# A gated linear unit on one core: handing out row pairs to partitions in another order

## The chip, the cores and the metric

The kernel runs on one core of one Trainium2 chip. The metric is device time in microseconds (us), the median of several executions; lower is better. Before the change it is 934.0 us, the median of three runs from 933.32 to 934.62 us.

## The reference

```python
def setup_inputs():
    return {
        "x": np.random.randn(8192, 8192).astype(np.float32),
    }

def reference(x: np.ndarray) -> np.ndarray:
    a, b = np.split(x, 2, axis=-1)
    return a * (1 / (1 + np.exp(-b)))
```

A row of x has 8,192 float32 values (32 KiB). Its second half is put through a sigmoid and multiplied into its first half, which gives a row of 4,096 values (16 KiB). Each output row depends on one input row alone, so it doesn't matter which partition of the on-chip memory a row passes through, as long as it is stored to the place that belongs to it. The kernel must read 268.44 MB and write 134.22 MB.

## The kernel before

A tile is 256 rows. Each of the 128 partitions holds two neighbouring rows of it (R = 2), called a row pair below: 64 KiB of input, 32 KiB of output. There are 32 tiles and two slots each for input and output.

```python
    R = 2
    SLOTS = 2
    n_tiles = n_rows // (P * R)
    x_t = x.rearrange("(n p r) m -> n p (r m)", p=P, r=R)
    out_t = out.rearrange("(n p r) m -> n p (r m)", p=P, r=R)

    pool = ctx.enter_context(tc.tile_pool(name="io", bufs=1))
    xs = [pool.tile([P, R * n_cols], fp32, name=f"x_sb{k}") for k in range(SLOTS)]
    os = [pool.tile([P, R * half], fp32, name=f"o_sb{k}") for k in range(SLOTS)]
    # ... cut: helpers for the waits
    for i in range(n_tiles):
        # ... cut: bookkeeping
        rows = xs[i % SLOTS].rearrange("p (r h m) -> p r h m", r=R, h=2)
        packed = os[i % SLOTS].rearrange("p (r m) -> p r m", r=R)

        load = nc.sync.dma_start(out=xs[i % SLOTS], in_=x_t[i])
        # ... cut
        if 0 < i < n_tiles - 1:
            parts = [(slice(0, R), slice(0, half))]
        else:
            w = half // 2
            parts = [
                (slice(r, r + 1), slice(c * w, (c + 1) * w)) for r in range(R) for c in range(2)
            ]
        def store(cols):
            ins = nc.scalar.dma_start(out=out_t[i, :, cols], in_=os[i % SLOTS][:, cols])
            now["stores"].append(ins)

        chunks = []
        for k, (r, c) in enumerate(parts):
            b = rows[:, r, 1, c]
            sig = nc.scalar.activation(out=b, in_=b, func=SIG)
            mul = nc.vector.tensor_mul(out=packed[:, r, c], in0=rows[:, r, 0, c], in1=b)
            # ... cut: which waits are kept
            chunks.append(slice(r.start * half + c.start, r.start * half + c.stop))
            if i == n_tiles - 1 and k > 0:
                store(chunks[k - 1])
        store(chunks[-1] if i == n_tiles - 1 else slice(0, R * half))
```

Loads are issued from SyncE, stores from ScalarE. A load goes into the slot of the tile two before it, so it waits for that tile's multiply. The last tile is stored in four parts of 1 MiB; every other tile is one load of 8 MiB and one store of 4 MiB. What is cut only decides which semaphore waits are written out, moves the first load ahead of the start-up, and shortens the closing sequence; the change touches none of it.

Of the kernel before, what the change touches and what calls it, by code (L numbers as in the profile page):

```python
# [1 line left out]

# [4 lines left out]


def _tiles(ctx, tc, x, out):

    nc = tc.nc
    P = nc.NUM_PARTITIONS  # L20
    DEP = mybir.DependencyInfo(mybir.DependencyClass.Sync, mybir.DependencyReason.DATA)
    fp32 = mybir.dt.float32
    SIG = mybir.ActivationFunctionType.Sigmoid

    n_rows, n_cols = x.shape
    half = n_cols // 2
    R = 2
    SLOTS = 2
    n_tiles = n_rows // (P * R)
    x_t = x.rearrange("(n p r) m -> n p (r m)", p=P, r=R)  # L30
    out_t = out.rearrange("(n p r) m -> n p (r m)", p=P, r=R)

    pool = ctx.enter_context(tc.tile_pool(name="io", bufs=1))
    xs = [pool.tile([P, R * n_cols], fp32, name=f"x_sb{k}") for k in range(SLOTS)]
    os = [pool.tile([P, R * half], fp32, name=f"o_sb{k}") for k in range(SLOTS)]

    def implied(later, *earlier):
        for e in earlier:
            tc.declare_no_dep(later.ins, e.ins, reason="follows from the waits that are kept")

    gone = [{k: [] for k in ("loads", "sigs", "muls", "stores")} for _ in range(SLOTS)]
    last_stores = [[] for _ in range(SLOTS)]
    for i in range(n_tiles):
        old = gone[i % SLOTS]
        freed = last_stores[i % SLOTS]
        now = {k: [] for k in old}
# [4 lines that stand above are left out]
        implied(load, *old["loads"], *old["sigs"])  # L51
        now["loads"].append(load)
# [6 lines that stand above are left out]
                (slice(r, r + 1), slice(c * w, (c + 1) * w)) for r in range(R) for c in range(2)  # L59
            ]  # L60
        def store(cols):
            ins = nc.scalar.dma_start(out=out_t[i, :, cols], in_=os[i % SLOTS][:, cols])  # L62
            now["stores"].append(ins)

        chunks = []
# [4 lines that stand above are left out]
            implied(sig, *old["sigs"], *old["muls"], *old["loads"])  # L70
            implied(mul, *old["muls"], *old["loads"], *now["loads"])
            by_sigmoid = i % 2 == 1 and len(parts) == 1
            implied(mul, *(s for s in old["stores"] if by_sigmoid or s not in freed))
            if by_sigmoid:
                for s in freed:
                    tc.add_manual_dep(sig.ins, s.ins.name, DEP, reason="frees the output slot")
            tc.keep_in_program_order(sig)
            now["sigs"].append(sig)
            now["muls"].append(mul)
# [4 lines that stand above are left out]
        for s in now["stores"]:  # L84
            implied(s, *old["loads"], *old["sigs"], *old["muls"], *now["loads"], *now["sigs"])
        for k in old:
            old[k] += now[k]
        last_stores[i % SLOTS] = now["stores"]


def _launch_early(nc):

    SP = mybir.EngineType.SP
    entry, body = (b.instructions for b in nc.main_func.blocks[:2])
    load = next(i for i in body if i.engine == SP and i.opcode == "DMACopy")
    assert not load.sync_info.on_wait
    body.remove(load)
    where = next(k for k, i in enumerate(entry) if i.engine == SP and i.opcode == "Drain")  # L100
    entry.insert(where, load)


def _close_on_sync(nc):

    SP, POOL = mybir.EngineType.SP, mybir.EngineType.Pool  # L110
    ACT = mybir.EngineType.Activation
    block = nc.main_func.blocks[2].instructions
    waits = block[0]
    assert waits.engine == SP and waits.opcode == "Drain" and len(waits.sync_info.on_wait) > 1
    pool = [i for i in block if i.engine == POOL]
    drain1, gather1, release1, reset, clear, drain2, gather2, release2 = pool
    assert reset.is_reset_sema and clear.opcode == "ISA"
    others = [i for i in block[1:] if i.engine != POOL]
    arrive = [i for i in others[: len(others) // 2] if i.opcode == "Drain"]
    assert len(arrive) == 4  # L120
    body = nc.main_func.blocks[1].instructions
    last = [i for i in body if i.engine == ACT and i.opcode == "DMACopy"][-1].sync_info.on_update[0].id
    final = [w for w in waits.sync_info.on_wait if w.id == last]
    assert len(final) == 1

    def event(engine, wait, update=()):
        return mybir.InstEventSemaphore(
            name=nc.get_next_instruction_name(),
            engine=engine,
            debug=waits.debug,  # L130
            sync_info=mybir.SyncInfo(on_wait=[wait], on_update=list(update)),
        )

    n = len(block)
    for lo, hi in ((reset.reset_range_start, last), (last + 1, reset.reset_range_stop)):
        if lo < hi:
            nc.gpsimd.sem_clear(range(lo, hi))
    clears = block[n:]
    assert clears and all(i.opcode == "ISA" for i in clears)
    back = mybir.SyncUpdate(  # L140
        sync_type="semaphore",
        id=last,
        ant_name=final[0].ant_name,
        update_mode="sem-sub-imm",
        update_value=final[0].wait_value,
        update_reg=None,
    )
    block[:] = [
        *arrive,
        drain1,  # L150
        gather1,
        *(event(POOL, w) for w in waits.sync_info.on_wait if w.id != last),
        reset,
        *clears,
        drain2,
        event(SP, final[0], [back]),
    ]


@with_exitstack  # L160
def kernel(
    ctx: ExitStack,
    tc: tile.TileContext,
    x: bass.AP,
    out: bass.AP,
):
    nc = tc.nc
    with ExitStack() as pools:
        _tiles(pools, tc, x, out)
    tc.close()  # L170
    tc.compile()
    _launch_early(nc)
    _close_on_sync(nc)


# [1 line left out]
_INS = ['x']  # L177
_OUTS = [((8192, 4096), 'float32')]


# [23 lines left out]
```

## Time and profile before

| | before |
|---|---|
| time, median of 3 | 934.0 us |
| span of the profiled execution | 931.7 us |
| sigmoid on ScalarE, full tile of 128 x 8,192 | 7.03 us (30 of them) |
| multiply on VectorE, full tile | 8.69 us (30 of them) |
| load, from issue to landing (median of 32) | 42.2 us |
| store of 4 MiB, from issue to landing (median of 31) | 34.7 us |
| chain that ended last | DMA 73%, DVE 15%, ACT 12% |

In the page of a profile, a busy digit is the busy share of one of 40 equal slices of the span, in tenths. The DMA row is the mean over the core's 16 DMA engines. q1 is the queue of the loads and q10 that of the stores: number of packets, megabytes, and the time that the packets took as a share of 16 engines over the span. The chain is followed back from the last instruction: at each step to what released it. A wait line names who waited for whom, the total in us, how often, and the longest.

### The profile page before, as it was taken

Reading aid. Unit: us, or ns where it says so; the run is one execution under the profiler, and the core shown is the slowest. Engines: PE = TensorE matmul, PEld = TensorE weight load, DVE = VectorE, ACT = ScalarE, POOL = GpSimd, SP = SyncE. Lnnn points to the kernel's source line nnn. Section 1 sums busy time; section 2 is a strip of 40 time slices with the busy share of each in tenths; the row PEclk is TensorE's granted clock in tenths of the full one; section 3 lists DMA queues with packets and bytes.
Section 4 is the critical chain, followed back from the end, with each engine's and each line's share of the span. In section 5 each row is a group of like instructions: output and inputs, shape, how many; then the busy total and the mean of one; then the engine's idle time right before and its main releaser. Section 6 shows DMA issues by size and latency. Waiting matters only on the chain.

```text
span 931.7 us, 247 instructions
## 1 busy us (share of the span) xinstructions
DVE 278.7 (30%) x38; ACT 227.1 (24%) x39; POOL 0.2 (0%) x4
## 2 busy tenths in 40 slices
DVE  0333213333133331233312333123331233312333
ACT  1323330233311333113331133311333113332033
POOL 0000000000000000000000000000000000000000
DMA  9999999999999999999999999999999999999999
GB/s 405 428 450 428 422 456 405 450 428 428 450 418 438 428 436 442 428 428 450 447 408 428 442 459 428 413 460 411 450 428 425 453 408 447 428 428 450 425 430 405
DMA packets 9649, 402.67 MB, mean 432 GB/s; under 512 B 1072, under 2 KB 1072, under 8 KB 1072
## 3 DMA queue, kind: packets, MB, share of 16 engines
q1 hardware_dynamic: 4608, 268.44, 66.6%
q10 hardware_dynamic: 5040, 134.22, 33.4%
q14 instruction: 1, 0.01, 0.0%
HBM read 268.44 MB, written 134.22 MB: 432 GB/s over the span
## 4 chain that ended last, share of the span: by engine, by line
DMA 73%; DVE 15%; ACT 12%; issue 0%; ACTq 0%
DMA x_sb<-in_x_dram 73%; DVE o_sb L69 15%; ACT x_sb L68 12%; ACTq L62 0%; ACTq L68 0%
## 5 line engine op out<-in xcount | busy, mean ns | idle before, releaser
L69 DVE TENSOR_TENSOR o_sb<-x_sb 128x8192 f32<-128x8192 f32 (+1 forms) x38 | 278.7, 7344 | 647.1 <-ACT x_sb L68 647.1
L68 ACT ACTIVATE x_sb<-x_sb 128x8192 f32<-128x8192 f32 (+1 forms) x38 | 225.8, 5952 | 695.6 <-DMA x_sb<-in_x_dram 694.4
L68 ACT ACT_TABLE_LOAD x1 | 1.3, 1283 | 0.8 <-PEq L188 0.8
L188 POOL MEMSET const-bfloat16-1.0<- 128x1 bf16 x1 | 0.1, 102 | 0.0
L188 POOL MEMSET const-uint8-127<- 128x1 uint8 x1 | 0.1, 102 | 0.0
L188 POOL MEMSET const-float32-0.0<- 128x1 f32 x1 | 0.1, 99 | 0.2 <-issue 0.2
L188 POOL MEMSET const-float32-1.0<- 128x1 f32 x1 | 0.1, 99 | 0.0
## 6 DMA issues: line engine op xcount, KB each, us to landing
out_dram<-o_sb ACTq DMA_DIRECT2D x31, 4096.0 KB, 34.7
out_dram<-o_sb ACTq DMA_DIRECT2D x4, 1024.0 KB, 5.6
x_sb<-in_x_dram SPq DMA_DIRECT2D x32, 42.2
```

The costliest lines, as they stand in the source:

```text
L68: sig = nc.scalar.activation(out=b, in_=b, func=SIG)
L69: mul = nc.vector.tensor_mul(out=packed[:, r, c], in0=rows[:, r, 0, c], in1=b)
L188: nc = _bacc.Bacc("TRN2", target_bir_lowering=False, num_devices=1)
```

## The change

Within a tile, partition p takes row pair 16 (p mod 8) + p div 8 where it took row pair p. Loads and stores use the same rule, so every output row comes out where it did. With p = 8 a + b, the partition's row pair is 16 b + a: partitions 0 to 7 hold row pairs 0, 16, 32, ..., 112, partitions 8 to 15 hold 1, 17, ..., 113, and so on.

The aim: the transfers are done by 16 DMA engines. If engine a serves the eight partitions from 8 a on, one after the other, then the sixteen engines read sixteen neighbouring row pairs at a time, one contiguous megabyte of memory, and step on to the next megabyte together[...]. The access pattern of the tensor in memory gets one dimension more for it, 16 x 8 x run where it was 128 x run; that of the on-chip tile stays 128 x run.

```diff
@@ -26,9 +26,10 @@
     half = n_cols // 2
     R = 2
     SLOTS = 2
+    ENGINES = 16
     n_tiles = n_rows // (P * R)
-    x_t = x.rearrange("(n p r) m -> n p (r m)", p=P, r=R)
-    out_t = out.rearrange("(n p r) m -> n p (r m)", p=P, r=R)
+    x_t = x.rearrange("(n b a r) m -> n a b (r m)", a=ENGINES, b=P // ENGINES, r=R)
+    out_t = out.rearrange("(n b a r) m -> n a b (r m)", a=ENGINES, b=P // ENGINES, r=R)
 
@@ -59,7 +60,7 @@
         def store(cols):
-            ins = nc.scalar.dma_start(out=out_t[i, :, cols], in_=os[i % SLOTS][:, cols])
+            ins = nc.scalar.dma_start(out=out_t[i, :, :, cols], in_=os[i % SLOTS][:, cols])
             now["stores"].append(ins)
```

## The prediction

> **What bounds the kernel now.** I read the page first: how busy each engine is, the DMA rows and the queue table.
>
> ```profile
> DVE 278.7 (30%) x38; ACT 227.1 (24%) x39; POOL 0.2 (0%) x4
> ...
> DMA  9999999999999999999999999999999999999999
> ...
> DMA packets 9649, 402.67 MB, mean 432 GB/s; under 512 B 1072, under 2 KB 1072, under 8 KB 1072
> ## 3 DMA queue, kind: packets, MB, share of 16 engines
> q1 hardware_dynamic: 4608, 268.44, 66.6%
> q10 hardware_dynamic: 5040, 134.22, 33.4%
> ```
>
> The compute engines are idle more than two thirds of the time; the 16 DMA engines are never idle. The queue table gives the cost of one packet. The load queue's 4,608 packets are 32 loads x (128 + 16): 4,096 packets of data, 64 KiB each (268.44 MB / 4,096), one to a partition, and 16 tiny ones per load. They take 0.666 x 16 x 931.7 us = 9,929 engine-us, or 2.424 us each. The store queue moves as many row pairs at 32 KiB: 0.334 x 16 x 931.7 / 4,096 = 1.216 us. The trace's packet records are just as flat: the median load packet is 2.418 us and 98% lie between 2.418 and 2.440; every 32 KiB store packet is 1.213 to 1.216. That is 65,536 B / 2.418 us = 27.1 GB/s for each engine, x 16 = 434 GB/s.
>
> Next the busy time by windows two tiles long (columns: window, its length, DVE, ACT, POOL, PEclk, DMA share, GB/s), and the chain that ended last (start, length, what):
>
> ```profile
> 116.00:174.00 58.00, 17.43 (x3) 14.06 (x2) 0.00 (x0) 1.00 1.00 434
> 582.00:640.00 58.00, 17.17 (x3) 14.06 (x2) 0.00 (x0) 1.00 1.00 433
> ```
>
> ```profile
> 102.88 7.04 ACT x_sb L68
> ...
> 109.94 8.70 DVE o_sb L69
> 118.66 42.09 DMA x_sb<-in_x_dram
> ...
> 160.84 7.04 ACT x_sb L68
> ```
>
> Two tiles take 160.84 - 102.88 = 57.96 us, 28.98 each. One tile costs an engine 8 load and 8 store packets, 8 x 2.418 + 8 x 1.213 = 29.05 us. The two agree: a tile lasts as long as an engine's sixteen packets, and the chain's sigmoid and multiply lie beside other transfers. Last the waits:
>
> ```profile
> ACT x_sb L68 <- DMA x_sb<-in_x_dram: 694.4, 32, 22.3
> ...
> SPq L50 <- DVE o_sb L69: 859.9, 30, 31.7
> ```
>
> ScalarE waits some 22 us per tile for a load, so compute has that much slack; and a load is issued only when the multiply two tiles back has freed its slot, which leaves roughly one to two loads in the queue. So the time is (packets per engine) x (time of a packet), and the change can act only through the packet's time or the spread of packets over engines.
>
> [...]
>
> **The change, part by part.** Removed and added: no instruction, byte or packet. A run in DRAM is still 64 KiB (loads) or 32 KiB (stores), so still 4,096 data packets per queue; sigmoid and multiply are indifferent to which row pair a partition holds, and load and store permute alike. Waits stay.
>
> Moved, first: the order in HBM. Where an engine holds partitions 8a to 8a+7 in order, the sixteen engines would at any step b read row pairs 16 b to 16 b + 15, one run of 1 MiB, instead of runs spread over 8 MiB. What is that worth? [...] The exceptions are 32 packets of 2.6 to 3.5 us: the first of 15 engines, one more of each engine about 34.5 us later, when the first store begins, and a single one. In the two groups they are about 0.8 us too long. Removing both groups would save 1.6 us. That is the ceiling, 0.2%.
>
> Moved, second: the engines' shares. The DRAM pattern's slowest dimension is now a, of size 16. [...]
>
> [...] a load packet takes 2 x 2.418 = 4.84 us, a store packet 2 x 1.213 = 2.43. A tile is then 8 x (4.84 + 2.43) = 58.1 us; 32 tiles 1,859; with the 934.0 - 32 x 29.05 = 4 us at the ends, 1,863 us. This is lockstep, the worst.
>
> It is softened by offsets. If an engine trails its partner by d us within a packet, both are alone for d in each, so the cycle of a load and a store is 7.26 - 2 d. In the trace 12 of 16 engines begin their first packet within 0.2 us of each other: at d = 0.2 the cycle is 6.86, a tile 54.9, the whole 1,760. [...] Sharing evenly, nothing makes d grow or shrink.
>
> [...] opposite phases help more: one engine stores while the other loads. Of a load's 2.418 us, 1.213 runs alone and 1.205 at half rate: 1.213 + 1.213 + 2.41 = 4.84 us per cycle, 38.7 a tile, 1,240 in all.
>
> [...]
>
> **The rivals.** *Nothing happens.* [...] For it: all packet sizes and waits are the same[...]. [...] It would give 932 to 936 us. *Locality helps.* For it: the 32 long packets; against it: the other 4,064. 932 at best. *Fewer engines.* If only the a loop of one side were spread differently, say 8 engines, packets would stay at 2.42 us and each engine would have 16 per tile: also 1,860[...]. [...] *Compute takes over.* It needs 15.8 us of a 29 us tile; no.
>
> **Range and chances.** I give 0.13 to no effect (about 934), 0.12 to partners that drift apart (about 1,000), 0.27 to partly opposite phases (1,240 to 1,600) and 0.48 to near lockstep (1,600 to 1,863). Half of this lies below about 1,600, the heaviest part above; I take 1,640. From 1,030 to 1,870 holds 8 in 10. Faster by over 2% is impossible while a packet takes 2.418 us; 0.01 for what I haven't thought of. Within 2%: 0.14. Slower: 0.85.
>
> **What would show it.** Packets: still 4,608 and 5,040, and DMA tenths still 9, but 220 to 330 GB/s instead of 434, with load packets of 4 to 5 us; the two queues' shares of 16 engines still near 66 and 33%. A tile of 45 to 58 us in the chain, load landings from 42.2 to some 80 us, store landings from 34.7 to some 65, ScalarE's wait for loads up by nearly the whole difference, DVE and ACT busy unchanged. I am wrong if packets stay at 2.42 us with 434 GB/s[...], if they stay at 2.42 with half the engines idle (fewer engines), or if long packets turn up in the loads alone[...].

## The result, and the profile after

The changed kernel takes 1,503.2 us, the median of six runs from 1,440.1 to 1,550.8 us; the kernel before took 933.3 us beside it (six runs, 933.1 to 934.6). The medians stand 1.61 to 1. The comparison with an interval gives a ratio of 1.548 [1.544, 1.552]; like every ratio below, it counts only runs within 1.5% of the fastest of their kernel, and so rests on the two lowest of the six. The predicted time was 1,640 us with a range of 1,030 to 1,870. The changed kernel also varies by 7.7% from run to run, where the kernel before varies by 0.2%.

The page of the changed kernel, with the rows that answer to those shown of before (the profiled execution is the second shortest of the six, 1,449.2 us of span):

```profile
DVE 278.7 (19%) x38; ACT 227.0 (16%) x39; POOL 0.2 (0%) x4
...
DMA  9999999999999999999999999999999999999996
...
DMA packets 9650, 402.67 MB, mean 278 GB/s; under 512 B 1073, under 2 KB 1073, under 8 KB 1073
...
q1 hardware_dynamic: 4608, 268.44, 74.8%
q10 hardware_dynamic: 5040, 134.22, 24.4%
```

Nothing was added: as many packets on each queue, as many bytes, VectorE and ScalarE as busy as before in microseconds. The DMA engines are still busy throughout, yet they move 278 GB/s instead of 432. So every packet must take longer. Loads: 0.748 x 16 x 1,449.2 us / 4,096 = 4.23 us, 1.75 times the 2.42 of before. Stores: 0.244 x 16 x 1,449.2 / 4,096 = 1.38 us against 1.216, 1.14 times. The packet records agree: the mean load packet is 4.231 us, the mean 32 KiB store packet 1.374 us.

Two windows of the changed kernel (window, length, DVE, ACT, POOL, PEclk, DMA share, GB/s), the first with loads alone, the second one tile long in the steady part:

```profile
2.00:45.00 43.00, 0.00 (x0) 2.04 (x2) 0.00 (x0) 1.00 0.99 206
764.00:809.00 45.00, 8.69 (x1) 7.03 (x1) 0.00 (x0) 1.00 1.00 284
```

Where only loads run the rate is worst, 206 GB/s. Before the first store begins, the median load packet of the changed kernel takes 5.12 us, 2.12 times the 2.418 before. With stores in between, the rate is better: 284 GB/s in the second window.

The chain that ended last, two tiles of the steady part (start, length, what):

```profile
277.30 7.04 ACT x_sb L69
...
284.36 8.70 DVE o_sb L70
...
293.63 29.67 another core or an unknown queue
...
323.32 7.04 ACT x_sb L69
...
330.38 8.70 DVE o_sb L70
...
339.65 30.26 another core or an unknown queue
...
370.00 7.04 ACT x_sb L69
```

The first tile shown lasts 323.32 - 277.30 = 46.0 us, against 29.0 before. The line "another core or an unknown queue" stands where the chain of before has the load. On a one-core kernel it can't be another core; the waits say what it is:

```profile
ACT x_sb L69 <- DMA x_sb<-in_x_dram: 1209.1, 32, 41.2
...
SPq L51 <- DVE o_sb L70: 1338.7, 30, 52.6
```

ScalarE's wait for loads grew from 694.4 to 1,209.1 us, by 514.7 of the span's 517.5. As before, 32 waits for 32 loads; only their length differs.

### The profile page after: what moved, and what is told of

It reads as the page before. It is cut to its first block, busy times and chain, and to the rows that moved or that the text cites. A ratio compares the mean times of both kernels' runs of the same rounds, so it can differ in the third digit from the quotient of the medians.

```text
span 1449.2 us, 247 instructions
## 1 busy us (share of the span) xinstructions
DVE 278.7 (19%) x38; ACT 227.0 (16%) x39; POOL 0.2 (0%) x4
## 3 DMA queue, kind: packets, MB, share of 16 engines
q1 hardware_dynamic: 4608, 268.44, 74.8%
q10 hardware_dynamic: 5040, 134.22, 24.4%
## 4 chain that ended last, share of the span: by engine, by line
another core or an unknown queue 61%; DVE 19%; ACT 15%; DMA 3%; ACTq 1%; issue 0%
DVE o_sb L70 19%; ACT x_sb L69 15%; DMA x_sb<-in_x_dram 3%; ACTq L63 1%; ACTq L69 0%
## 5 line engine op out<-in xcount | busy, mean ns | idle before, releaser
L69 ACT ACTIVATE x_sb<-x_sb 128x8192 f32<-128x8192 f32 (+1 forms) x38 | 225.7, 5949 | 1210.6 <-DMA x_sb<-in_x_dram 1209.1
## 6 DMA issues: line engine op xcount, KB each, us to landing
out_dram<-o_sb ACTq DMA_DIRECT2D x31, 4096.0 KB, 54.5
x_sb<-in_x_dram SPq DMA_DIRECT2D x32, 72.8
```

## The experiments

The theory is that of the prediction: with the 16 x 8 split the packets of two engines, called partners, collide and take about twice as long, whatever the order in memory. That engines meet in this way was the author's supposition: no view used here names a packet's engine or a place where two would meet. So the theory has to show itself in the times of the packets. The rivals put the loss in the interleaved order in memory, in the pattern's third dimension, or in a straight split as such.

### Interleaved in memory, but in blocks of four partitions

```diff
-    x_t = x.rearrange("(n b a r) m -> n a b (r m)", a=ENGINES, b=P // ENGINES, r=R)
+    x_t = x.rearrange("(n b a r) m -> n a b (r m)", a=BLOCKS, b=P // BLOCKS, r=R)   # BLOCKS = 32
```

The output is stored with the same pattern.

> Loads and stores in the order row pair 32 b + a for partition p = 4 a + b: an access pattern of 32 x 4 in memory, again interleaved and again one dimension more than before[...]. Theory ([...]the order in memory is harmless): [...]packets of 2.42 and 1.21 us, 931 to 936 us. Rival 1 (the interleaved order in memory collides in HBM): still interleaved, so long packets, 1,300 to 1,550 us. Rival 2 (any pattern with one dimension more is slow): 1,440 to 1,550 us.

Measured: 934.1 us (13 runs, 933.8 to 934.9) beside 933.6, ratio 1.0005 [0.9997, 1.0013]. The queue table of this run:

```profile
DMA packets 9650, 402.67 MB, mean 432 GB/s; under 512 B 1073, under 2 KB 1073, under 8 KB 1073
...
q1 hardware_dynamic: 4608, 268.44, 66.6%
q10 hardware_dynamic: 5040, 134.22, 33.3%
```

These are the shares of the kernel before, from a pattern that is 32 x 4 in memory and hands out row pairs 32 apart. So neither the third dimension nor interleaving as such costs anything here (ratio 1.0005). It brings nothing either: the two groups of 16 long packets are still there (2.9 to 3.7 us at the start, 3.2 to 3.5 us about 34.5 us later), so this order of the reads doesn't remove them.

### Split 16 x 8, but in the old order in memory

```diff
-    x_t = x.rearrange("(n b a r) m -> n a b (r m)", a=ENGINES, b=P // ENGINES, r=R)
+    x_t = x.rearrange("(g a h b r) m -> g h a b (r m)", a=ENGINES, h=2, b=P // ENGINES, r=R)
-        load = nc.sync.dma_start(out=xs[i % SLOTS], in_=x_t[i])
+        load = nc.sync.dma_start(out=xs[i % SLOTS], in_=x_t[i // 2, i % 2])
```

The output goes the same way. This is the opposite half of the change.

> A 16 x 8 pattern in which each group of 8 partitions walks through 8 neighbouring row pairs (512 KiB in one piece, groups 1 MiB apart, two tiles interleaved), so the order in memory is much as before the change while the pattern is split 16 x 8. Theory: the split decides; 1,440 to 1,560 us, load packets of 4 to 5.1 us. Rival 1 (the interleaved order in memory is what costs): near 934 us, packets of 2.42 us.

Measured: 1,468.6 us (four runs, 1,426.7 to 1,500.8), ratio 1.536 [1.528, 1.543].

```profile
DMA packets 9649, 402.67 MB, mean 280 GB/s; under 512 B 1072, under 2 KB 1072, under 8 KB 1072
...
q1 hardware_dynamic: 4608, 268.44, 74.8%
q10 hardware_dynamic: 5040, 134.22, 24.6%
```

The page of the changed kernel again, but for 280 and 278 GB/s, though each group of eight partitions walks through memory in one piece. The packets last as long, too: loads 4.21 us on average, stores 1.38 us. The groups lie 1 MiB apart in memory here; that this distance costs something of its own isn't excluded by this run alone, but it would have to cost just what the changed kernel loses. So the loss comes with the 16 x 8 split, in both orders that were run (ratios 1.548 and 1.536), and the interleaved order that was run with another split costs nothing (1.0005). The order of the change itself was not run without its split.

### Loads alone, stores alone

```diff
# loads only                                # stores only: the same for out_t
-    x_t = x.rearrange("(n p r) m -> n p (r m)", p=P, r=R)
+    x_t = x.rearrange("(n b a r) m -> n a b (r m)", a=16, b=P // 16, r=R)
```

Here the rows of a tile leave in another order than they should; every transfer is otherwise as in the two kernels.

> Only the loads take the new order, stores keep the old one; rows of a tile leave in another order. Theory: loads collide with loads[...]. With 5.12 us per load packet, as the first two tiles of the changed kernel show, the loads alone need 32 x 8 x 5.12 = 1,311 us; stores find room meanwhile: 1,320 to 1,480 us, store packets near 1.21 us. Rival[...]: the stores queue up too, 1,500 us or more.

Measured: 1,544.8 us (1,530.6 to 1,558.2), ratio 1.646 [1.639, 1.653]; the time is outside what the theory expected and in the rival's.

```profile
DMA packets 9649, 402.67 MB, mean 261 GB/s; under 512 B 1072, under 2 KB 1072, under 8 KB 1072
...
q1 hardware_dynamic: 4608, 268.44, 76.7%
q10 hardware_dynamic: 5040, 134.22, 23.0%
```

The mean load packet is 4.63 us, the mean store packet 1.39 us rather than 1.21.

> Only the stores take the new order, loads keep the old one; rows of a tile leave in another order. Theory: stores of two partners collide only while both store; 2 x 1.213 us in lockstep would give 8 x (2.418 + 2.43) x 32 = 1,241 us, opposite phases 934 us; I expect 950 to 1,150 us with load packets at 2.42 us. Rival[...]: a store also meets the loads of other engines, load packets longer than 2.6 us, over 1,150 us.

Measured: 981.5 us (973.7 to 988.6), ratio 1.048 [1.042, 1.055].

```profile
DMA packets 9649, 402.67 MB, mean 414 GB/s; under 512 B 1072, under 2 KB 1072, under 8 KB 1072
...
q1 hardware_dynamic: 4608, 268.44, 65.7%
q10 hardware_dynamic: 5040, 134.22, 33.7%
```

Over three quarters of the load packets still take 2.418 us (mean 2.496) and the mean store packet is 1.276. Over 1.3 us are 1% of the store packets in the first half of the execution and 15% in the second. Stores in the new order hardly touch the loads: 2.496 us on average against 2.424. So the rival, by which a store also meets the loads of other engines and makes their packets longer than 2.6 us, doesn't fit this run, in spite of the first run's total. The loads carry the loss: alone they cost as much as loads and stores together, or more (611 us against 570 between the medians). Why the old stores are worse company for the new loads than the new stores is taken up below.

### The place in on-chip memory

A plain copy without sigmoid and multiply, over 64 partitions, and without the early first load and the short closing sequence. The two kernels differ in one number.

```diff
-    P = nc.NUM_PARTITIONS
+    P = 64
+    LO = 32        # second run: LO = 0
+    SLOTS = 6
     # ... cut: tiles of 64 rows; compute and waits are gone
+        here = xs[i % SLOTS][LO : LO + P]
+        nc.sync.dma_start(out=here, in_=x_t[i])
+        nc.scalar.dma_start(out=out_t[i], in_=here[:, :half])
```

> No compute and half of the tile: 128 tiles of 64 rows, loaded to 64 partitions and the first half of each row stored straight from there, a plain copy with the same bytes; partitions 32 to 95. [...] Theory[...]: 128 x 4 x (1.213 + 0.61) = 933 us and some us at the ends, 930 to 960 us[...]. Rival (a straight split is slow in itself[...]): over 1,300 us.

> The same copy with nothing changed but the place: partitions 0 to 63[...]. Theory[...]: 1,350 to 1,650 us as with the change, at most twice e5, 32 KiB load packets of 2.0 to 2.6 us. Rival[...]: the same as e5.

Measured: 940.6 us (940.5 to 941.8) on partitions 32 to 95, 1,464.2 us (1,449.8 to 1,470.6) on 0 to 63; against the kernel before 1.0075 [1.006, 1.009] and 1.567 [1.556, 1.579]. The queue tables, first of partitions 32 to 95:

```profile
DMA packets 20484, 402.70 MB, mean 429 GB/s; under 512 B 4096, under 2 KB 4096, under 8 KB 4096
...
q1 hardware_dynamic: 10240, 268.44, 66.4%
q10 hardware_dynamic: 10240, 134.23, 33.5%
```

and of partitions 0 to 63:

```profile
DMA packets 20484, 402.70 MB, mean 277 GB/s; under 512 B 4096, under 2 KB 4096, under 8 KB 4096
...
q1 hardware_dynamic: 10240, 268.44, 73.2%
q10 hardware_dynamic: 10240, 134.23, 26.6%
```

The same rows of memory, the same packets, the same instructions; only the place on the chip moved by 32 partitions. 429 GB/s became 277, and the shares moved from near two to one, the proportion of the bytes, towards those of the changed kernel (74.8 and 24.4%). Packets of 32 KiB took 1.216 us on average in the first and 2.081 us in the second. In both the shares add up to 99.8% of 16 engines or more, so no engine is left out. The place in on-chip memory alone can make a loss like that of the change: 1,464.2 us against 940.6.

### Without stores

```diff
-        store(chunks[-1] if i == n_tiles - 1 else slice(0, R * half))
+        if i == n_tiles - 1:
+            store(chunks[-1])
```

Only the last tile's rows are written; the rest of the output is left out. Once in the changed kernel, once in the kernel before:

> The changed kernel with the stores of all tiles but the last left out. Theory: with nothing but loads, partners always collide and take 5.12 us a packet, as in the changed kernel's first tiles: 32 x 8 x 5.12 = 1,311 us and some 20 us at the ends, 1,320 to 1,350 us. [...] Rival (partners drift apart in time and avoid each other): well under 1,200 us.

> The kernel before with the stores of all tiles but the last left out: the measure for e7. 32 x 8 x 2.42 = 620 us and some 20 us at the ends, 630 to 650 us; e7 should be 2.1 times this[...], and less than 1.9 times if partners drift apart.

Measured: 1,317.2 us (1,311.5 to 1,322.8) with the change, 656.5 us (653.7 to 656.9) without: 2.01 to 1. The page of the changed kernel without stores:

```profile
GB/s 223 191 223 191 223 191 223 191 223 191 223 191 223 191 223 191 223 193 221 193 221 193 221 193 221 197 217 197 217 197 217 197 217 209 205 213 201 219 195 191
DMA packets 5184, 272.63 MB, mean 207 GB/s; under 512 B 576, under 2 KB 576, under 8 KB 576
...
q1 hardware_dynamic: 4608, 268.44, 98.5%
```

Between 191 and 223 GB/s in every slice, with every one of the 4,096 load packets above 4.2 us (mean 5.07, median 5.12). The time is 3 us below what was expected of it. With loads alone the packets stay long from end to end; nothing shortens them over 1.3 ms. The kernel before without stores came out 7 us above what was expected of it: its mean load packet is 2.466 rather than 2.42 us, and its DMA share sinks at the end where the last tile is computed and stored:

```profile
DMA  9999999999999999999999999999999999999986
...
DMA packets 5184, 272.63 MB, mean 416 GB/s; under 512 B 576, under 2 KB 576, under 8 KB 576
...
q1 hardware_dynamic: 4608, 268.44, 96.4%
```

So the ratio misses the expected 2.1, but 2.01 is above the 1.9 or less of drifting partners.

## Why the prediction was right, point by point

**Bound.** Read rightly: the time is packets per engine times the time of a packet. After, 8 x (4.231 + 1.374) = 44.8 us a tile, x 32 = 1,435 of the 1,449 us profiled. (One reading was slightly off: 99% of the load packets of before lie between 2.418 and 2.440 us, not 98%.) The range from 1,030 to 1,870 us covers nearly every packet time from that of before to twice as much, so that the time lies in it is a weak test; packets that last longer with the same bytes are the stronger one.

**Order in memory, at most 1.6 us.** Nothing speaks against it: the 32 x 4 order gained nothing that its interval shows.

**Shares of the engines.** That the split gives each engine other partitions, and that two engines then collide, was inferred, and no view shows it. The 16 x 8 pattern is slow in either order (1,503.2 and 1,468.6 us), and the 32 x 4 pattern is not (934.1 us). The two copies show, as far as times can, that the place in on-chip memory counts: 64 partitions at 32 run at 429 GB/s, at 0 they run at 277. What is shown is that the loss comes with this split, and that the place in on-chip memory alone makes a loss of the same kind. That the split makes packets of two engines collide is a reading that fits both; which partitions an engine carries, and which engines would be partners, is not shown.

**A colliding packet at twice its time.** 4.84 us was predicted, 5.12 measured: at that pace two engines together move 2 x 65,536 B / 5.12 us = 25.6 GB/s, 6% less than one engine before the change (27.1).

**How far the packets collide.** The mis-sized term, the store's above all. Lockstep got the most weight, with 7.26 us for a load and a store (4.84 and 2.43); measured is 4.231 + 1.374 = 5.61 us, between that and the 4.84 of opposite phases, and the time fell in the 1,240 to 1,600 that had 0.27. A store of twice its time, 2.43 us, hardly occurs: in the first nine tenths of the changed kernel's execution one of 3,539 store packets of 32 KiB takes over 1.7 us. Nor does the new order of the stores explain their 1.374 us, since stores in the old order took 1.39 us beside the new loads. And the packets don't stay as they start, as the prediction's offset d would have them ("nothing makes d grow or shrink"): the mean load packet falls from 4.81 us in the first tenth to between 4.07 and 4.19 from the fourth on.

The run without stores gives a simpler sum. There every load packet is long: 256 x 5.12 = 1,311 us, measured 1,317 in all. In the profiled executions the stores add 1,449.2 - 1,318.5 = 131 us, where their packets fill 0.244 x 1,449 = 354 us of each engine: 37%. Between the medians they add 186 us. Beside the stores the mean load packet is shorter, 4.231 us instead of 5.07; by the author's estimate from these sums, a load speeds up while its partner stores. In the kernel before, where the load packet takes 2.424 us with stores and 2.466 without, they add 933.3 - 656.5 = 277 us.

**Stores beside loads.** The opposite phases of the prediction suppose that a store doesn't hinder a partner's load. The nearest that was run are new stores with old loads, where loads grew by 3%, to 2.496 us.

**Drift to 1,000 us (0.12), fewer engines, no effect (0.13).** None came. Fewer engines would have left packets at 2.42 us, and the two queues' shares, which add up to 99.2%, at about half.

**What the profile would show.** 278 GB/s lies in 220 to 330, the mean load packet in 4 to 5 us; the tile, 44.8 us on average, falls just short of 45 to 58. Loads land after 72.8 us (some 80 said) and stores after 54.5 (some 65). Wrong was that the queues' shares stay near 66 and 33%: this supposed loads and stores stretched alike, and they went to 74.8 and 24.4%. The shift is itself the sign that loads stretched, by 75%, and stores far less. With that, one sign of being wrong came close: long packets in the loads alone; stores grew by only 13%. The two copies, with the same rows of memory, speak for the place in on-chip memory all the same; but in these runs it is the loads that carry the loss (1,544.8 us with the loads alone in the new order, 981.5 with the stores alone).

**What stays open.** First, old stores with new loads take 1,545 us, more than new stores with new loads, though the ranges overlap (1,531 to 1,558 and 1,440 to 1,551). In the profiled executions the old stores add 1,544.5 - 1,318.5 = 226 us to the loads, against 131 for the new. The loads differ as well: the middle half of their packets lies within 4.55 to 4.64 us beside the old stores, and within 3.95 to 4.51 beside the new ones. That colliding new stores push partners out of step was the author's guess; but long packets of new stores, over 1.7 us, are hardly to be seen before the last tenth (1 of 3,539, then 38), so it is not shown. Nor does any run explain why stores in the old order take 1.39 us beside the new loads. Second, the spread of the runs. Without stores the four runs lie within 0.9%, with old stores within 1.8%, with old loads and new stores within 1.5%, with both new the six within 7.7%, so the spread comes with new loads and new stores together; that engines stand in other phases to each other from run to run is a guess that no run tests.

## What to carry to other kernels

The access pattern on the side of the memory decided here more than where the bytes go: as many packets of the same size took 2.42 us with 32 x 4 and 4.2 us with 16 x 8. The author's reading, which no view shows, is that it also decides which DMA engine carries which partitions. In a kernel bound by its DMA engines, as this one, measure a split before keeping it (here 128 and 32 x 4 on the side of the memory took 933 and 934 us, 16 x 8 took 1,503). To see such a loss, divide a queue's share of the 16 engines by its packets: if the time of a packet grows while bytes and packets stay the same, test the place in on-chip memory before the order in memory.

## What the runs showed of the hardware that was not expected

A 64 KiB load packet of the 16 x 8 split, with loads alone in the queues, takes 5.12 us, 2.12 times its 2.418 and not the estimated two. Beside loads of that split (4.63 us on average) a 32 KiB store takes 1.39 us instead of 1.213 even when it keeps the old order. A copy over only 64 partitions runs at 429 GB/s, within 1% of the time of the kernel over 128, if they are partitions 32 to 95; on 0 to 63 it runs at 277. Both were expected before they ran. With the loads in the new order, moving the stores to it as well did no harm: the medians are 1,545 and 1,503 us, with ranges that overlap.
